# One store for the mLSTM state, and q evictions and output gates as woven tasks, in a one-core encoder step

## The chip, the cores and the metric

The kernel runs on one core of one Trainium2 chip. The metric is the device time of one execution in microseconds. The engines are named as in the profile: PE (TensorE, matmuls; PEld is its weight load), DVE (VectorE), ACT (ScalarE), POOL (GpSimd), and SP (SyncE), which here only issues DMAs. Each engine works off its own instructions in the order in which they stand in the program, and waits on semaphores for what they read.

## The reference: what is computed

One inference step of a two-layer encoder for a prompt of 1024 frames and a sample of 32 frames (1056 columns together), in float32, model width 1024. Layer 0 is an mLSTM (8 heads, key width 64, value width 128, chunks), layer 1 a sliding-window attention (16 query heads, 2 key/value heads). Both are followed by a SwiGLU feed-forward of width 2816. After each sub-layer comes x <- LayerNorm(alpha x + sublayer(x)).

The part that matters here is the mLSTM mixer:

```python
q, k, v, o, ig, fg = jnp.split(x @ w_in, A_SPLITS, axis=-1)
...
# per chunk, with the gates folded into d, w_inter, w_end, decay, m
qk = jnp.einsum('bhtd,bhsd->bhts', q, k) * d
num = w_inter[..., None] * jnp.einsum('bhtd,bhde->bhte', q, C0) + jnp.einsum('bhts,bhse->bhte', qk, v)
den = w_inter * jnp.einsum('bhtd,bhd->bht', q, n0) + jnp.sum(qk, -1)
h = num / jnp.maximum(jnp.abs(den), jnp.exp(-m))[..., None]
C_new = decay[..., None, None] * C0 + jnp.einsum('bhs,bhsd,bhse->bhde', w_end, k, v)
n_new = decay[..., None] * n0 + jnp.einsum('bhs,bhsd->bhd', w_end, k)
...
h = h * lax.rsqrt(jnp.mean(h * h, -1, keepdims=True) + HEAD_NORM_EPS)
h = h.reshape(B, T, H * M_DV) * g_norm * jax.nn.sigmoid(o)
return h @ w_out, C, n, m
```

The last C, n and m of the prompt and of the sample are outputs, beside the two y and some rows of K and V.

## The kernel before, in words

**Tiles.** The 1056 columns are cut into three groups of 384, 384 and 288 for the projections, and into nine chunks (eight of 128 columns for the prompt, one of 32 for the sample) for the mLSTM. The heads go in four pairs. Each float32 operand is split into a high and a low part, and each product is three matmuls (lines 582 to 584); these are called dense here. `d` is their PSUM tile, a ring of three banks in this stage. `wr` is a loaded weight of 512 KB, `wh` and `wl` its parts (lines 387 and 392; `oh` are further places for such parts), `sx` the parts of x.

**The mixer's stages.** For pair j the kernel projects q (three groups, each evicted to `qT` by ACT, line 894), k (evicted to `kT` by DVE, line 899) and v (nine chunks, evicted to `vt`). With v of pair 0 come the gates' raw values; `gate_task` turns them into rows of m and of weights (`scrm`, `scrw` in DRAM, lines 974 and 993), into columns, and last into the decays (PE line 1015). `mlstm` then runs one `item` per pair and chunk, 36 in all. An item loads `nm` and `wib` by broadcast DMAs from `scrm` and `scrw` (lines 1042 and 1046), copies q (POOL 1055, 1059), adds the mask to `nm` (POOL 1061), takes the exponential (ACT 1065), multiplies scores S = k q (PE 1075) by it into `p` (DVE 1080), forms H and the new state on PE (1098, 1100, 1102), updates C and n together as `Cn`, 128 x 129 (DVE 1122), normalises, and transposes the result (PE 1162) into `act`. Items 7 and 8 of a pair end the prompt's and the sample's state, and are stored with two DMAs each: C (128 rows of 128 elements, line 1130) and n (128 rows of one element, line 1131). After the four pairs `proj_o` projects the output gates o, takes the sigmoid by exponentials and logarithms, and multiplies it into `act`.

**What sets the order.** The program is straight-line code and the order on each engine is fixed when it is built. Some work is written as tasks (generators); `Weave` steps a task when a planner, `Clock`, thinks that its next instruction could start by the time PE gets there. `Clock` keeps a time for each engine and tile from fixed costs of each instruction. The stages around the tasks are plain code: `project` issues a group's dense matmuls and calls the tasks in between. `wv.until` and `wv.drain` step only tasks until a condition holds, so no dense matmul is placed meanwhile. Three such places bear on the change. Line 1192 holds q of pair j >= 2 until all nine items of pair j-2 are placed, because `qT` has two buffers. `begin` (line 1178) drains the gate task, opens a pool in the gates' room and starts `mlstm`; it is called after q and k of pair 1. And each `proj_o` pair waits for its items. SP issues all loads and stores in one queue, in the order in which they were placed.

Of the kernel before, what the change touches and what calls it, by code (L numbers as in the profile page):

```python
# [17 lines left out]
P = 128  # L18
# [6 lines left out]
HEADS = 8  # L25
# [39 lines left out]
class Clock:  # L65
# [70 lines left out]
    def see(self, i, *_):  # L136
# [13 lines left out]
        if op == "DMACopy":  # L150
# [291 lines left out]
def kernel(ctx: ExitStack, tc: tile.TileContext, A, O):  # L442
# [144 lines left out]
    def psbank():  # L587
        return new(psx[1][0], "d", [P, 512], F32, bufs=psx[1][1])

    def psdense(g):  # L590
        return psbank()[:, : GRP[g][1]]
# [13 lines left out]
    def project(u, g):  # L605

        ps = psdense(g)
        gemm(ps, wcols(u), xcols(g))
        return ps
# [419 lines left out]
    def mlstm():  # L1029
# [3 lines left out]
        def item(j, c):  # L1033
# [94 lines left out]
            else:  # L1128
                k = "p" if c == 7 else "s"
                nc.sync.dma_start(O[k + "_C"][2 * DK * j : 2 * DK * (j + 1), :], Cn[:, :DV])  # L1130
                nc.sync.dma_start(O[k + "_n"][2 * DK * j : 2 * DK * (j + 1), :], Cn[:, DV : DV + 1])
# [46 lines left out]
    def begin():  # L1178
        nonlocal pa2, task
        wv.drain(gtask)  # L1180
# [9 lines left out]
    for j in range(PAIRS):  # L1190
        if j > 1:
            wv.until(lambda: mst["done"] >= 9 * (j - 1))
        alloc_pair(j)
        if j:
            for g in range(3):
                proj_q(j, g)
            W.done(U_Q[j])
            for g in range(3):
                proj_k(j, g)
            W.done(U_K[j])  # L1200
        else:
            for g in range(3):
                proj_q(j, g)
                if g == 0:
                    W.split_to(U_V[0][0])
                if g == 2:
                    W.done(U_Q[j])
                    W.split_to(U_V[0][1])
                proj_k(j, g)
            W.done(U_K[j])  # L1210
# [7 lines left out]
    def proj_o(m, g, release):  # L1218
# [3 lines left out]
        if release:  # L1222
            W.done(U_O[m])
        t, r = scratch(m % 2, n)
# [26 lines left out]
    def scratch(i, n):  # L1251
        return [new(pa2, tag, [P, 384], bufs=2)[:, :n] for tag in ("sg", "sr")]
# [5 lines left out]
    wv.drain(task)  # L1258
    gn = base.tile([P, KT], F32, name="gn")
# [5 lines left out]
    def scratch(i, n):  # L1265
        return zz[:, 2 * i, :n], zz[:, 2 * i + 1, :n]

    for g in range(3):
        for m in range(6, 8):
            proj_o(m, g, False)  # L1270
# [713 lines left out]
def _arrays(i):  # L1984
# [49 lines left out]
    "p_C": (HEADS * DK, DV),  # L2034
    "p_n": (HEADS * DK, 1),
# [3 lines left out]
    "s_C": (HEADS * DK, DV),  # L2039
    "s_n": (HEADS * DK, 1),  # L2040
# [39 lines left out]
```

## Time and profile before

| | us |
|---|---|
| median of 3 runs | 2326.53 (2323.96 to 2331.42) |
| the profiled execution | 2327.41 |
| its span | 2325.6 |
| PE busy | 2239.0 (96%) |
| DVE busy | 1519.5 (65%) |
| ACT busy | 1030.2 (44%) |
| POOL busy | 793.7 (34%) |

Times in the profile are in us from the start of the span. A row of a timeline has the start, the duration, the engine and line, the operation with output and inputs, and in brackets how long the engine idled before it and what ended that. The stretch view gives each engine's busy time in a stretch, PE's granted clock (1.00 is full speed), the mean busy share of the 16 DMA engines, and what they moved. Roughly, the mixer's projections and mLSTM fill the first 400 us, layer 0's output projection and feed-forward the time to 1200, the attention 1250 to 1550, and layer 1's feed-forward the rest.

### The profile page before, as it was taken

The page shows a single profiled execution, that of the slowest core. Times are in us where ns is not written, and L with a number is a line of the kernel's source. Part 1 is how long each engine was busy: PE and PEld are TensorE (multiplying, and loading weights), DVE is VectorE, ACT ScalarE, POOL GpSimd, SP SyncE. Part 2 cuts the span into 40 slices and gives each one's busy share as a digit, 9 for nine tenths or more (in the row PEclk, how much of TensorE's full clock was granted, in tenths as well). Part 3 has the DMA queues.
Part 4 walks back from the last instruction along what each step waited for, and adds up shares of the span by engine and source line. Part 5 has one row for each costly group of instructions (what it writes and reads, how often), then busy time and mean ns, then how long its engine had stood idle before and what let it go on. Part 6 is the DMA issues. An engine that isn't in the chain of part 4 may idle for free.

```text
span 2325.6 us, 44258 instructions
## 1 busy us (share of the span) xinstructions
PE 2239.0 (96%) x17224; PEld 2182.8 (94%) x17224; DVE 1519.5 (65%) x3001; ACT 1030.2 (44%) x2300; POOL 793.7 (34%) x792
## 2 busy tenths in 40 slices
PE   8979999999999999999999899889999999999997
PEld 8868999999999999999998788889999999999997
DVE  4445456767766565666677767767766666566666
ACT  3334345555444444322257666656544444331233
POOL 1223210001545445444202545410244545444410
PEclk9979999999999999999999989989999999999999
DMA  4223221402434343698323100331244434389711
GB/s 144 67 49 53 64 29 55 139 19 73 167 121 167 139 158 121 236 328 264 118 82 110 48 31 21 105 115 37 74 167 158 149 126 161 103 287 329 246 57 66
DMA packets 165090, 289.71 MB, mean 125 GB/s; under 512 B 15824, under 2 KB 120840, under 8 KB 164880
## 3 DMA queue, kind: packets, MB, share of 16 engines
q1 hardware_dynamic: 160528, 282.56, 36.9%
q10 hardware_dynamic: 4352, 4.33, 0.5%
q8 instruction: 135, 2.21, 0.4%
q14 instruction: 75, 0.61, 0.1%
HBM read 203.89 MB, written 82.94 MB: 123 GB/s over the span
## 4 chain that ended last, share of the span: by engine, by line
PE 78%; DVE 8%; ACT 6%; DMA 4%; issue 3%; POOL 1%; SPq 0%; ACTq 0%; POOLq 0%; DVEq 0%
PE d L582 9%; PE d L583 9%; PE d L584 9%; PE A L582 8%; PE A L584 8%; PE A L583 8%; PE B L582 6%; PE B L583 6%; PE B L584 6%; PE ln L642 1%; PE T L1856 1%; PE H L1098 1%; ACT wh L387 1%; DMA hs_x<-z 1%; PE H L1100 1%
## 5 line engine op out<-in xcount | busy, mean ns | idle before, releaser
L392 POOL TENSOR_TENSOR wl<-wr,wh 128x512 fp32r<-128x512 f32 x406 | 574.2, 1430 | 915.7 <-ACT wh L387 831.9
L387 ACT CAST wh<-wr 128x512 fp32r<-128x512 f32 (+1 forms) x531 | 319.6, 617 | 477.0 <-DVE wr L361 264.7
L582 PE MATMUL A<-sx,wh 128*128 128x264 f32 x1280 | 364.5, 285 | 3.4 <-ACT z L1510 2.9
L583 PE MATMUL A<-sx,wh 128*128 128x264 f32 x1280 | 363.1, 284 | 0.0
L584 PE MATMUL A<-sx,wl 128*128 128x264 f32 x1280 | 363.1, 284 | 0.0
L582 PE MATMUL d<-sx,wh 128*128 128x264 f32 (+2 forms) x1092 | 345.9, 317 | 10.0 <-ACT sx L612 6.0
L583 PE MATMUL d<-sx,wh 128*128 128x264 f32 (+2 forms) x1092 | 337.4, 309 | 0.7 <-DVE sx L613 0.6
L584 PE MATMUL d<-sx,wl 128*128 128x264 f32 (+2 forms) x1092 | 336.5, 308 | 0.1
L582 PEld LDWEIGHTS A<-sx,wh 128*128 128x128 f32 x1280 | 240.6, 188 | 4.3 <-ACT z L1510 3.3
L584 PEld LDWEIGHTS A<-sx,wl 128*128 128x128 f32 x1280 | 241.2, 188 | 0.0
L583 PEld LDWEIGHTS A<-sx,wh 128*128 128x128 f32 x1280 | 240.7, 188 | 0.0
L582 PE MATMUL B<-ex,wh 128*128 128x264 f32 x832 | 236.5, 284 | 0.0
L583 PE MATMUL B<-ex,wh 128*128 128x264 f32 x832 | 236.0, 284 | 0.0
L584 PE MATMUL B<-ex,wl 128*128 128x264 f32 x832 | 235.8, 283 | 0.0
L582 PEld LDWEIGHTS d<-sx,wh 128*128 128x128 f32 x1092 | 210.4, 193 | 12.5 <-ACT sx L612 6.2
L583 PEld LDWEIGHTS d<-sx,wh 128*128 128x128 f32 x1092 | 210.4, 193 | 2.6 <-DVE sx L613 1.8
L584 PEld LDWEIGHTS d<-sx,wl 128*128 128x128 f32 x1092 | 209.8, 192 | 0.4 <-DVE wl L392 0.4
L582 PE MATMUL d<-sx,ex 128*128 128x264 f32 x612 | 177.3, 290 | 0.0
L584 PE MATMUL d<-sx,ex 128*128 128x264 f32 x612 | 173.7, 284 | 1.1 <-DVE ex L392 1.1
L1851 POOL TENSOR_SCALAR s<-s,st 128x256 f32<-128x256 f32 (+1 forms) x144 | 124.1, 876 | 146.1 <-DVE st L1848 126.6
L583 PE MATMUL d<-sx,ex 128*128 128x264 f32 x612 | 173.7, 284 | 0.0
L1376 DVE TENSOR_TENSOR z<-z 128x528 fp32r<-128x528 f32 x136 | 117.9, 880 | 69.8 <-ACT z L1374 69.4
(274 smaller groups left out, 5822.4 us busy)
## 6 DMA issues: line engine op xcount, KB each, us to landing
wr<-in_gu SPq DMA_DIRECT2D x96, 512.0 KB
hs_x<-z SPq DMA_DIRECT2D x72, 528.0 KB
hs_t<-z SPq DMA_DIRECT2D x64, 528.0 KB
sx<-hs_x SPq DMA_DIRECT2D x112, 264.0 KB
sx<-hs_t SPq DMA_DIRECT2D x64, 264.0 KB
ex<-hs_t SPq DMA_DIRECT2D x64, 264.0 KB
wr<-in_dn SPq DMA_DIRECT2D x32, 512.0 KB
ex<-hs_x SPq DMA_DIRECT2D x32, 264.0 KB
```

Source lines behind the costliest of these rows:

```text
L387: self.nc.scalar.copy(hi, r)
L392: eng.tensor_sub(lo, r, hi.bitcast(F32))
L582: nc.tensor.matmul(out, ah, bh, start=start and k == 0, stop=False, **kw)
L583: nc.tensor.matmul(out, ah, bl, start=False, stop=False, **kw)
L584: nc.tensor.matmul(out, al, bh, start=False, stop=stop and k == last, **kw)
L642: nc.tensor.matmul(t[:, :w], onesm[:], x[:, i, :], start=(i == 0), stop=(i == 1))
L1098: nc.tensor.matmul(ph[:L, h, :], p[:L, h, :L], vt[j][:L, c, h, :], start=True, stop=C is None)
L1100: nc.tensor.matmul(ph[:L, h, :], qw[:, h, :L], C[:], start=False, stop=True)
L1376: clk.sooner(2 * N4, hi).tensor_sub(lo.bitcast(F32R), buf(s), hi)
L1851: nc.gpsimd.tensor_scalar_mul(p[:R, h, lo:256], p[:R, h, lo:256], st[:R, 2, h : h + 1])
L1856: nc.tensor.transpose(pt[:nk, i, h, :R], p[:R, h, c : c + nk], ident[:R, :R])
```

## The change

It has four parts. The state matrix C and vector n, which lie together in `Cn`, leave in one store of 128 rows of 129 elements, and the host cuts them apart. The eviction of q is a task that waits for pair j-2 and holds its PSUM bank until it has run; the tiles of the pair are allocated in it. `begin` is a task that runs as soon as the gate task has ended. The output gates are a task for each group, which holds its PSUM bank until the first exponential, and holds its two scratch tiles to the end. Beside that three constants of the planner are other: a DMA whose rows are one element is costed at 8.5e-5 of the unit in which others have 0.1 to 0.39, an issue of a DMA takes 0.4 us of its engine in place of 0.06, and a result of 8 or 64 partitions no longer lets the next instruction of its engine overlap.

```diff
-            rate = 0.39 if row >= 2048 else 0.30 if row >= 1024 else 0.2 if row >= 512 else 0.1
+            rate = 0.39 if row >= 2048 else 0.30 if row >= 1024 else 0.2 if row >= 512 else 0.1 if row > 4 else 8.5e-5
             self.pipe = max(start + 1.3, self.pipe) + n / rate / 1e6
-            self.free[e] = start + 0.06
+            self.free[e] = start + 0.4
...
-            self.free[e] = end - self.LAP.get(e, 0.0)
+            part = outs and outs[0].ap[0][1] in (HEADS, 64)
+            self.free[e] = end + (0.014 if part else -self.LAP.get(e, 0.0))
...
-    def psbank():
-        return new(psx[1][0], "d", [P, 512], F32, bufs=psx[1][1])
...
+    def psbank(hold=False):
+        p, bufs = psx[1]
+        wv.until(ring(p, "d", bufs).open)
+        return new(p, "d", [P, 512], F32, bufs=bufs, hold=hold)
...
     def proj_q(j, g):
         t0, n = GRP[g]
-        ps = project(U_Q[j], g)
-        nc.scalar.copy(qT[j][:, t0 : t0 + n], ps)
+        t, ps = project(U_Q[j], g, True)
+
+        def out():
+            yield At("Activation", [ps], when=lambda: mst["done"] >= 9 * (j - 1))
+            if g == 0:
+                alloc_pair(j)
+            nc.scalar.copy(qT[j][:, t0 : t0 + n], ps)
+            release(psx[1][0], "d", t)
+
+        wv.launch(out())
 
     def proj_k(j, g):
         t0, n = GRP[g]
         ps = project(U_K[j], g)
+        if g == 0:
+            wv.until(lambda: j in qT)
...
-                nc.sync.dma_start(O[k + "_C"][2 * DK * j : 2 * DK * (j + 1), :], Cn[:, :DV])
-                nc.sync.dma_start(O[k + "_n"][2 * DK * j : 2 * DK * (j + 1), :], Cn[:, DV : DV + 1])
+                nc.sync.dma_start(O[k + "_Cn"][2 * DK * j : 2 * DK * (j + 1), :], Cn[:])
...
     def begin():
         nonlocal pa2, task
-        wv.drain(gtask)
+        yield At("SP", when=lambda: gtask not in wv.tasks)
...
     for j in range(PAIRS):
-        if j > 1:
-            wv.until(lambda: mst["done"] >= 9 * (j - 1))
-        alloc_pair(j)
...
             gtask = wv.launch(gate_task())
+            wv.launch(begin())
             W.ahead = True
         mst["ready"] = j + 1
+        proj_v(j)
         if j == 1:
-            begin()
-        proj_v(j)
+            wv.until(lambda: task)
...
+    def gate_out(m, g, bank, ps):
+        n = GRP[g][1]
+        rooms = [ring(pa2, tag, 2) for tag in ("sg", "sr")]
+        yield At("Activation", [ps], room=rooms)
+        both = [new(pa2, tag, [P, 384], bufs=2, hold=True) for tag in ("sg", "sr")]
+        t, r = (x[:, :n] for x in both)
+        nc.scalar.activation(t, ps, AF.Exp, scale=-1.0)
+        release(psx[1][0], "d", bank)
...
+        yield At("DVE", lambda: [t, h[:]], when=lambda: mst["done"] >= 9 * (m // 2 + 1))
+        nc.vector.scalar_tensor_tensor(h, h, gnorm[:, m : m + 1], t, op0=ALU.mult, op1=ALU.mult)
+        for tag, x in zip(("sg", "sr"), both):
+            release(pa2, tag, x)
...
     for m in range(6):
-        wv.until(lambda: mst["done"] >= 9 * (m // 2 + 1))
         for g in range(3):
-            proj_o(m, g, g == 2)
+            bank, ps = project(U_O[m], g, True)
+            gating.append(wv.launch(gate_out(m, g, bank, ps)))
+        W.done(U_O[m])
```

The order of instructions moves in three places of which the prediction speaks. The numbers in the rows are those of the tiles; the lines of the changed kernel are some 1 to 12 higher.

**The start of the mLSTM, on SP.** `Cs`, `nm` and `wib` are the first items' loads, `wr` a weight. Before:

```order
L993 DMA scrw_213<-wi_799 8x288
L995 DMA out_p_m<-m_798 8x1
L996 DMA out_s_m<-m_798 8x1
L343 DMA wr_912<-in_wqk 128x1024
L343 DMA wr_1004<-in_wv 128x1024
L343 DMA wr_1020<-in_wv 128x1024
L1039 DMA Cs_1046<-in_state_cn 128x129
L1042 DMA nm_1048<-scrm_208 128x2x128
L1042 DMA nm_1052<-scrm_208 128x2x128
L1046 DMA wib_1054<-scrw_211 64x128 x2
```

and now:

```order
L344 DMA wr_893<-in_wqk 128x1024
L1005 DMA scrw_213<-wi_816 8x288
L1007 DMA out_p_m<-m_815 8x1
L1008 DMA out_s_m<-m_815 8x1
L1051 DMA Cs_947<-in_state_cn 128x129
L1054 DMA nm_949<-scrm_208 128x2x128
L1054 DMA nm_953<-scrm_208 128x2x128
L1058 DMA wib_955<-scrw_211 64x128 x2
L1054 DMA nm_960<-scrm_208 128x2x128
L1058 DMA wib_962<-scrw_211 64x128 x2
L1054 DMA nm_1036<-scrm_209 128x2x128
L1058 DMA wib_1038<-scrw_212 64x128 x2
```

The two loads of wv stood ahead of the first item; they now follow the fourth. On PE the last gate matmul (line 1015) has 27 more dense matmuls ahead of it than before, and the first S stands 24 dense matmuls behind it, where 138 stood.

**The turn from pair 0 to pair 1, on SP.** Before:

```order
L1042 DMA nm_1598<-scrm_210 32x2x32
L1046 DMA wib_1600<-scrw_213 64x32 x2
L1130 DMA out_p_C<-Cn_1626 128x128
L1131 DMA out_p_n<-Cn_1626 128x1
L343 DMA wr_1650<-in_wqk 128x1024
L343 DMA wr_1664<-in_wqk 128x1024
L1130 DMA out_s_C<-Cn_1705 128x128
L1131 DMA out_s_n<-Cn_1705 128x1
L1039 DMA Cs_1714<-in_state_cn 128x129
L1042 DMA nm_1716<-scrm_208 128x2x128
```

and now:

```order
L1054 DMA nm_1476<-scrm_210 32x2x32
L1058 DMA wib_1478<-scrw_213 64x32 x2
L1051 DMA Cs_1538<-in_state_cn 128x129
L1054 DMA nm_1540<-scrm_208 128x2x128
L1142 DMA out_p_Cn<-Cn_1562 128x129
L1054 DMA nm_1609<-scrm_208 128x2x128
L1058 DMA wib_1611<-scrw_211 64x128 x2
L1142 DMA out_s_Cn<-Cn_1649 128x129
L1054 DMA nm_1679<-scrm_208 128x2x128
L1058 DMA wib_1681<-scrw_211 64x128 x2
```

The first broadcast of pair 1 stands ahead of the state's stores, and the two weight loads have gone from here; they follow the fourth item of pair 1.

**The end of pair 0, on PE.** `ht` is an item's result; its transposition is an item's last work on PE, and the 128x32 one is the last of the pair. Before:

```order
L1102 MATMUL T_1687<-vt_228,ks_1674 64x129 x2
L1162 MATMUL T_1702<-ident,ht_1697 128x128 x2
L1162 MATMUL T_1736<-ident,ht_1734 128x32 x2
L582 MATMUL d_1753<-sx,oh_102_996 128x384
L583 MATMUL d_1753<-sx,oh_102_996 128x384
L584 MATMUL d_1753<-sx,oh_103_997 128x384
```

and now:

```order
L583 MATMUL d_1729<-wh_765,sx 32x256
L584 MATMUL d_1729<-wl_766,sx 32x256
L585 MATMUL d_1729<-wh_765,sx 32x256
L1173 MATMUL T_1733<-ident,ht_1717 128x32 x2
L1087 MATMUL S_1742<-qz_215,kT_790 128x256
L1089 MATMUL T_1744<-ident,kT_790 128x128
```

Before, v of pair 1 (32x256 is its last chunk) was used up, and the last transpositions followed each other with q of pair 2 behind them. Now the pair ends inside v of pair 1, and items of pair 1 are already under way. The order also differs in the attention stage; in the feed-forward stages PE's order is as it was.

More of the change, by code (lines that the diff above doesn't have):

```diff
@@ L1190, with proj_o @@
     for j in range(PAIRS):
-        if j > 1:
-            wv.until(lambda: mst["done"] >= 9 * (j - 1))
-        alloc_pair(j)
+        for g in range(3):
+            proj_q(j, g)
+            if not j and g == 0:
+                W.split_to(U_V[0][0])
+            if g == 2:
+                W.done(U_Q[j])
+                if not j:
+                    W.split_to(U_V[0][1])
+            if not j:
+                proj_k(j, g)
         if j:
             for g in range(3):
-                proj_q(j, g)
-            W.done(U_Q[j])
-            for g in range(3):
                 proj_k(j, g)
[L1200 to L1210, printed above, removed]
+        W.done(U_K[j])
+        if not j:
             gtask = wv.launch(gate_task())
+            wv.launch(begin())
             W.ahead = True
         mst["ready"] = j + 1
+        proj_v(j)
         if j == 1:
-            begin()
-        proj_v(j)
-    def proj_o(m, g, release):
+            wv.until(lambda: task)
+    def proj_o(m, g):
         n = GRP[g][1]
         ps = project(U_O[m], g)
-        if release:
-            W.done(U_O[m])
-        t, r = scratch(m % 2, n)
+        t, r = (zz[:, 2 * (m % 2) + i, :n] for i in range(2))
         nc.scalar.activation(t, ps, AF.Exp, scale=-1.0)
@@ L2038 @@
     "p_v": (P, P),
-    "s_C": (HEADS * DK, DV),
-    "s_n": (HEADS * DK, 1),
+    "s_Cn": (HEADS * DK, DV + 1),
     "s_m": (HEADS, 1),
```

35 lines of the change are left out of this document (21 added, 14 removed).

## The prediction

> **What bounds the kernel now.** I read the page first, then busy time by stretch, then who waits in the worst stretch, then SP's queue in order of time.
>
> ```profile
> span 2325.6 us, 44258 instructions
> PE 2239.0 (96%) x17224; PEld 2182.8 (94%) x17224; DVE 1519.5 (65%) x3001; ACT 1030.2 (44%) x2300; POOL 793.7 (34%) x792
> ```
>
> TensorE (PE) is the bound: 2239.0 of 2325.6 us. The order of instructions has 16,577 rows for PE before and as many after, of the same shapes, so the change cannot make PE's work smaller. It can only take away PE's idle time (86.6 us) and the time in which PE runs at a lower granted clock. The next question is how much of either lies where the change acts. The columns below are the stretch, its length, busy time and count of PE, PEld, DVE, ACT and POOL, the granted clock, the DMA share and GB/s.
>
> ```profile
> 95.00:110.00 15.00, 11.76 (x81) 10.78 (x80) 3.93 (x17) 4.09 (x14) 6.60 (x14) 0.89 0.30 92
> 110.00:135.00 25.00, 24.89 (x203) 22.61 (x201) 16.22 (x73) 10.65 (x43) 10.61 (x27) 1.00 0.12 28
> 135.00:140.00 5.00, 3.48 (x30) 2.59 (x30) 2.73 (x15) 3.10 (x13) 0.00 (x0) 1.00 0.06 13
> 140.00:160.00 20.00, 9.12 (x33) 5.40 (x32) 6.90 (x27) 4.96 (x18) 2.98 (x8) 0.55 0.58 86
> 160.00:170.00 10.00, 9.81 (x47) 8.57 (x48) 3.77 (x19) 3.74 (x14) 4.96 (x11) 0.71 0.16 45
> 170.00:215.00 45.00, 45.00 (x328) 40.91 (x327) 24.70 (x108) 20.00 (x76) 13.37 (x33) 1.00 0.29 34
> 215.00:230.00 15.00, 12.48 (x98) 10.78 (x98) 7.91 (x38) 6.19 (x26) 9.09 (x22) 1.00 0.36 114
> 230.00:400.00 170.00, 170.00 (x1175) 161.39 (x1175) 96.58 (x315) 74.83 (x219) 24.94 (x60) 1.00 0.20 47
> ...
> 1250.00:1550.00 300.00, 263.89 (x1718) 243.60 (x1718) 211.44 (x734) 194.46 (x575) 132.86 (x169) 0.91 0.21 67
> 1460.00:1470.00 10.00, 6.14 (x29) 5.08 (x27) 8.18 (x29) 6.03 (x17) 5.40 (x6) 0.66 0.33 107
> ```
>
> The mLSTM stage runs from about 93 to 326 us. PE idles there at three places only: 95 to 110, 135 to 160, 215 to 230. These are the starts of pair 0, pair 1 and pair 2. From 230 to 400 us it has no idle time at all, so what the change does to the output gates has nothing to win there. The last two rows are the attention stage, which the new constants of the planner reorder; more of it below.
>
> Idle time in the mLSTM stage: 3.24 + 0.11 + 1.52 + 10.88 + 0.19 + 2.52 = 18.5 us. Clock: a PE busy for 9.12 us at 0.55 does what takes 9.12 x 0.55 at full clock, so it loses 9.12 x 0.45 = 4.1 us; likewise 11.76 x 0.11 = 1.3 and 9.81 x 0.29 = 2.8. Together 8.2 us. **The whole that can be won here is 26.7 us.**
>
> Who waits in the worst of it, 138 to 160 us (engine, line, what it waited for, total, times, longest):
>
> ```profile
> POOL nm L1061 <- DMA nm<-scrm: 11.3, 1, 11.3
> DVE p L1080 <- ACT nm L1065: 9.0, 1, 9.0
> ACT nm L1065 <- POOL nm L1061: 8.5, 1, 8.5
> ...
> PE T L1162 <- DVE ht L1156: 4.2, 2, 2.6
> ```
>
> PE waits for p, p for nm on ACT, that for nm on POOL, and POOL for a DMA: the broadcast of -m into nm. Ahead of that (140 to 150) PE only follows the last two items of pair 0 with no dense work between them, since line 1192 lets q of pair 2 begin when pair 0 is done. SP's queue in that stretch (start, duration of the issue):
>
> ```profile
> 138.81 0.43 SPq L1131 DMA_DIRECT2D out_p_n<-Cn  x1
> ...
> 140.99 1.96 SPq L343 DMA_DIRECT2D wr<-in_wqk  x2
> ...
> 147.41 0.42 SPq L1131 DMA_DIRECT2D out_s_n<-Cn  x1
> ...
> 148.41 1.06 SPq L1042 DMA_DIRECT2D nm<-scrm  x2
> ...
> 158.17 0.72 POOL L1061 TENSOR_TENSOR nm<-nm,cmask 128x256 f32<-128x256 f32 x1 [11.30 <-DMA nm<-scrm]
> ...
> 160.19 1.23 PE L1098 MATMUL H<-vt,p 128*128 128x129 f32 x4 [5.71 <-DVE p L1080]
> ```
>
> ```profile
> 142.00:143.00 1.00, 0.29 (x1) 0.00 (x1) 1.00 (x2) 0.54 (x2) 0.00 (x0) 0.50 2.85 82
> 143.00:149.00 6.00, 3.58 (x14) 1.30 (x14) 3.10 (x19) 1.54 (x7) 0.15 (x2) 0.50 0.29 35
> 149.00:153.00 4.00, 3.16 (x10) 2.94 (x11) 0.82 (x4) 0.19 (x1) 0.00 (x0) 0.50 1.22 295
> 153.00:158.00 5.00, 1.48 (x5) 0.87 (x3) 0.00 (x0) 0.00 (x0) 0.00 (x0) 0.50 0.37 37
> ```
>
> Two weight loads of 512 KB were issued at 141 to 143 us, yet the DMA engines move 35 GB/s until 149, and only then 295 GB/s. After that again 37 GB/s until nm lands at 158. Each of the slow stretches (6 and 5 us) stands right behind one of the two stores of n, 128 rows of 4 bytes each. I read them as about 5.5 us of queue time per store. A weight load alone does not explain 35 GB/s.
>
> **The change part by part.**
>
> *One store for C and n.* Eight issues of this row go; the eight C stores get one column more.
>
> ```profile
> L1131 SPq DMA_DIRECT2D out_p_n<-Cn x4: 424/432/881, 138.8 to 317.4; - x4
> ```
>
> That is 8 x 0.43 = 3.4 us of SP's issuing time, off the path by itself. What counts is the queue behind: 2 x 5.5 = 11 us at the turn to pair 1, in which nm, wib and the weights stand still. The trace has no store of 516-byte rows. Its bounds are the 0.34 us issue of a C store (nothing more behind it) and the 5.5 us of an n store; by form it is nearest to the C store, whose 512-byte rows it exceeds by one element, so I take nothing. The Trainium skill (DMA: Bandwidth & Descriptors, Specifications) says the same of the two sizes in its own terms: full rate from 512 B on, below that a read-modify-write; no run here shows yet whether 516 bytes keep to it.
>
> *begin() as a task, after the gates; q evicted by tasks.* Before, the mLSTM of pair 0 waits for all of q and k of pair 1:
>
> ```profile
> 77.07 1.06 PE L1015 MATMUL T<-dec,sel 8*128 8x9 f32 x8
> ...
> 91.10 1.81 SPq L343 DMA_DIRECT2D wr<-in_wv  x2
> ...
> 93.44 0.94 SPq L1042 DMA_DIRECT2D nm<-scrm  x2
> ...
> 97.68 0.59 PE L1075 MATMUL S<-qz,kT 128*128 128x256 f32 x2
> ...
> 98.11 0.27 PE L1077 MATMUL T<-ident,kT 128*128 128x128 f32 x1
> ...
> 100.67 0.72 POOL L1061 TENSOR_TENSOR nm<-nm,cmask 128x256 f32<-128x256 f32 x1 [6.58 <-issue]
> ...
> 102.69 0.71 PE L1098 MATMUL H<-vt,p 128*128 128x129 f32 x4 [3.24 <-DVE p L1080]
> ```
>
> In the new order the last gate matmul (L1015) comes 27 dense matmuls later and the first S 24 dense matmuls behind it. A dense matmul takes 0.16 us (row below), so the gates end at about 77.1 + 4.3 + 1.1 = 82.5 and S stands at 86.3 instead of 97.7. The broadcasts now leave before the two wv loads, not behind them. Here nm took 100.67 - 93.44 = 7.2 us with 1.05 MB ahead of it, which at 349 GB/s (row below) is 3.0 us; so 4.2 us without. From the gates' end: 0.8 us to the issue (an estimate: the copy of the decays, the hand-over to SP and the issue of Cs ahead), 4.2 to nm on POOL, then 2.0 (100.67 to 102.69) to H, 7.0 us. On PE between: (24 + 9) x 0.16 + 0.9 for S and T = 6.2 us. So I expect a wait of 0.8 us there, where there were 3.2.
>
> ```profile
> 350.00:400.00 50.00, 50.00 (x310) 50.00 (x310) 31.13 (x62) 23.90 (x49) 0.00 (x0) 1.00 0.16 51
> 215.00:218.00 3.00, 2.68 (x23) 2.25 (x22) 1.70 (x8) 0.24 (x2) 0.02 (x1) 1.00 1.01 349
> ```
>
> At the turn to pair 1 the chain of pair 0 ends inside v of pair 1, so dense work covers the 140 to 150 stretch. The new wait is in q's eviction: it holds a PSUM bank until pair j-2 is done, and behind it on ACT stand the weight splits. With three banks, PE can run q's 72 matmuls (11.5 us) past that wait before it stops; before, it could run none. Cost nothing; if the chain were later than that by x, PE would stop for x.
>
> The two wqk loads (pair 3's) move behind four items of pair 1. They are used some 70 us later.
>
> *Output gates in tasks.* Same instructions in number, on ACT and DVE, under a PE that is full from 230 to 400. Nothing; if the cover went, the 18 evictions would show, at 0.49 us each 8.9 us:
>
> ```profile
> L1225 ACT ACTIVATE sg<-d x18: 411/492/495, 325.0 to 390.8; 128x384 f32<-128x384 f32 x12, 128x288 f32<-128x288 f32 x6
> ```
>
> *The planner's constants* (0.4 us for a DMA issue, no overlap behind results of 8 or 64 partitions) reorder the attention stage too, where PE idles 36.1 us and runs at 0.91. A gap such as 1460 to 1470 costs 3.9 us idle and 6.14 x 0.34 = 2.1 us of clock, 6 us. The new order may make or mend such gaps; the bounds are two more and two fewer, 12 us either way. I take nothing, since both orders have much the same dense work between the steps. The feed-forward stages keep PE's order.
>
> **The sum.** 26.7 us can be won. I leave 0.8 at pair 0, and 2 us each at pairs 1 and 2 for the 1 MB of weights that still passes among the broadcasts (pair 2's idle 2.5 us is the row for that). 26.7 - 4.8 = 22. The profiled execution took 2327.4 us (span 2325.6 and 1.8 around it): 2305.4. The median of the runs is 0.9 lower, so **2305 us**.
>
> **Rivals.**
>
> *The weights, not the n stores, hold the broadcasts.* For it: 1 MB stood ahead of nm at all three places, and pair 0 lost 3.24 + 1.3 = 4.5 us with no n store about. Against it: 35 GB/s behind n stores. If each turn keeps 4.5 us, 13.5 of the 26.7 stay, and the time is 2327.4 - 13.2 - 0.9 = 2313. The Trainium skill (DMA: Bandwidth & Descriptors, Queues, rings and completion order) has each DMA engine take descriptors in ring order, which is this rival's mechanism: a load on SP's queue delays whatever SP issues after it. The trace agrees in so far as nm lands only after the loads issued ahead of it.
>
> *Attention comes out better by two gaps*: 2293.
>
> *Slower: attention loses more gaps than the mLSTM stage wins.* Place 1250 to 1550, price 6 us a gap; from the fourth gap on (24 against 22) the gain is gone, and from the fifth it is measurably slower. Six give 2305 + 36 = 2341, with DVE (211 of 300 us) and ACT (194) too loaded to catch up. Against it: the steps keep their number, and the constants added are nearer to the measured 0.43 us issue than those replaced.
>
> *It does not do what it says*: the bank held for q stops PE as long as line 1192 did, so 135 to 170 keeps its 1.5 + 10.9 + 4.1 + 2.8 = 19 us, and the time is 2322. The new order speaks against it: pair 0's last transposes stand before the end of v of pair 1.
>
> **How the numbers follow.** The forecast has 0.67 (own range 2297 to 2314), the weights 0.13, better attention 0.08, no effect 0.06, slower 0.06. A measurement of this kernel tells 0.3% (7 us) from no change: below 2319.5 is faster. Faster: nearly all of the first three, 0.84; the same: no effect and a little of the weights' case, 0.10; slower 0.06. For 8 in 10 the range takes in two better gaps at one end and the weights' case with one worse gap at the other: 2291 to 2320.
>
> **What would show it.** Right: no PE wait over 1.5 us at L1098 at the starts of pairs 1 and 2; clock 1.00 from 110 to 230; nm on POOL within 5 us of its issue; first S near 86 us; the mLSTM's last item about 22 us earlier; the attention's idle within 12 us of 36. Wrong: broadcasts that still take 8 to 10 us without the n stores; PE waiting for a bank (ACT qT) at q of pair 2; an attention with 50 us of idle.

## The result and the profile after

The changed kernel takes **2296.57 us** (median of 4 runs, 2296.23 to 2298.87), the kernel before 2326.60 beside it (2323.96 to 2331.42). The ratio is 0.9871, 95% interval 0.9853 to 0.9888: 30.0 us faster. The forecast was 2305, with a range of 2291 to 2320. So the sign and the range hold, and the gain is 8 us larger than the sum gave.

The page of the changed kernel:

```profile
span 2294.8 us, 44265 instructions
PE 2226.5 (97%) x17224; PEld 2175.6 (95%) x17224; DVE 1520.1 (66%) x3005; ACT 1029.1 (45%) x2300; POOL 787.3 (34%) x788
```

PE has the same 17,224 matmul records. Its busy time is 12.5 us shorter, because more of it runs at full clock, and its idle time fell from 86.6 to 68.3 us. The same stretches of the mixer as in the prediction, with the columns named there:

```profile
95.00:110.00 15.00, 15.00 (x124) 14.01 (x121) 11.23 (x47) 6.92 (x27) 6.48 (x15) 1.00 0.41 118
...
135.00:140.00 5.00, 5.00 (x41) 4.34 (x40) 3.54 (x15) 2.13 (x9) 4.34 (x12) 1.00 0.08 22
140.00:160.00 20.00, 20.00 (x136) 18.70 (x135) 11.47 (x46) 9.99 (x34) 8.22 (x20) 1.00 0.34 94
160.00:170.00 10.00, 10.00 (x70) 9.14 (x69) 5.56 (x28) 5.49 (x23) 1.77 (x8) 1.00 0.01 2
...
215.00:230.00 15.00, 15.00 (x106) 13.00 (x103) 9.62 (x41) 7.56 (x26) 0.92 (x5) 1.00 0.30 87
230.00:400.00 170.00, 169.80 (x1169) 163.92 (x1169) 101.76 (x281) 78.74 (x207) 20.17 (x45) 1.00 0.21 62
...
1220.80:1577.20 356.40, 318.37 (x2164) 298.61 (x2163) 257.82 (x817) 229.43 (x642) 133.27 (x169) 0.92 0.19 62
```

Where PE idled for 18.5 us and lost 8.2 us of clock, nothing is left: 0.2 us of idle time in 305 us, and a clock of 1.00 throughout. The last row is the attention, from the first score to the last item of its output projection; in it 38.0 us are idle. Before, that stretch read:

```profile
1248.90:1607.70 358.80, 322.29 (x2176) 300.95 (x2177) 256.79 (x814) 230.17 (x639) 135.52 (x171) 0.92 0.19 61
```

That is 36.5 us of idle time in 358.8. Where the 30.8 us between the two spans went, by the first or last start of a tile in each trace:

| place | before | after | gained up to here |
|---|---|---|---|
| last exponential of an output gate | 390.8 | 363.6 | 27.2 |
| first up-projection of layer 0's feed-forward | 563.0 | 534.2 | 28.8 |
| first score of the attention | 1248.9 | 1220.8 | 28.1 |
| last item of the attention's output projection | 1607.7 | 1577.2 | 30.5 |
| end of the span | 2325.6 | 2294.8 | 30.8 |

The starts of pair 0 and pair 1 in the changed kernel, from its timeline (SP's queue, POOL and PE):

```profile
81.32 0.94 SPq L1054 DMA_DIRECT2D nm<-scrm  x2
...
81.36 1.05 PE L1027 MATMUL T<-dec,sel 8*128 8x9 f32 x8
...
85.02 0.73 POOL L1073 TENSOR_TENSOR nm<-nm,cmask 128x256 f32<-128x256 f32 x1 [3.02 <-issue]
...
86.69 0.59 PE L1087 MATMUL S<-qz,kT 128*128 128x256 f32 x2
...
88.54 0.61 PE L1110 MATMUL H<-vt,p 128*128 128x129 f32 x4
...
124.79 0.34 SPq L1142 DMA_DIRECT2D out_p_Cn<-Cn  x1
125.24 0.38 SPq L1054 DMA_DIRECT2D nm<-scrm  x1
...
130.53 0.35 SPq L1142 DMA_DIRECT2D out_s_Cn<-Cn  x1
130.99 0.37 SPq L1054 DMA_DIRECT2D nm<-scrm  x1
...
131.90 0.61 PE L1110 MATMUL H<-vt,p 128*128 128x129 f32 x4
```

The first nm is on POOL 3.7 us after its issue (3.1 and 3.5 us for the first of pairs 1 and 2), and no H has a wait in brackets. All of PE's waits of any size from 60 to 440 us (engine, line, what it waited for, total, times, longest):

```profile
PE T L1173 <- DVE small L1158: 0.2, 1, 0.2
```

What remained open is which part brought how much, why the gain is larger than the sum, and what the attention's order has to do with it.

### The profile page after: what moved, and what is told of

It reads as the page before. It is cut to its first block, busy times and chain, and to the rows that moved or that the text cites. A ratio compares the mean times of both kernels' runs of the same rounds, so it can differ in the third digit from the quotient of the medians.

```text
span 2294.8 us, 44265 instructions
## 1 busy us (share of the span) xinstructions
PE 2226.5 (97%) x17224; PEld 2175.6 (95%) x17224; DVE 1520.1 (66%) x3005; ACT 1029.1 (45%) x2300; POOL 787.3 (34%) x788
## 4 chain that ended last, share of the span: by engine, by line
PE 86%; DVE 5%; DMA 3%; ACT 3%; issue 2%; POOL 1%; POOLq 0%; ACTq 0%; SPq 0%; DVEq 0%
PE d L583 11%; PE d L584 11%; PE d L585 11%; PE A L583 9%; PE A L584 9%; PE A L585 9%; PE B L583 7%; PE B L584 7%; PE B L585 6%; PE T L1882 1%; PE ln L644 1%; PE O L1899 1%; PE H L1110 1%; PE psS L1863 1%; PE S L1087 1%
## 5 line engine op out<-in xcount | busy, mean ns | idle before, releaser
L393 POOL TENSOR_TENSOR wl<-wr,wh 128x512 fp32r<-128x512 f32 (+1 forms) x401 | 566.3, 1428 | 826.8 <-ACT wh L388 740.9
L583 PE MATMUL d<-sx,ex 128*128 128x264 f32 x596 | 172.7, 290 | 0.0
L585 PE MATMUL d<-sx,ex 128*128 128x264 f32 x596 | 169.2, 284 | 0.0
L584 PE MATMUL d<-sx,ex 128*128 128x264 f32 x596 | 169.2, 284 | 0.0
L1402 DVE TENSOR_TENSOR z<-z 128x528 fp32r<-128x528 f32 x136 | 112.3, 837 | 74.3 <-ACT z L1400 73.5
```

Of the source, the lines that this page charges most:

```text
L393: eng.tensor_sub(lo, r, hi.bitcast(F32))
L583: nc.tensor.matmul(out, ah, bh, start=start and k == 0, stop=False, **kw)
L584: nc.tensor.matmul(out, ah, bl, start=False, stop=False, **kw)
L585: nc.tensor.matmul(out, al, bh, start=False, stop=stop and k == last, **kw)
L1402: clk.sooner(2 * N4, hi).tensor_sub(lo.bitcast(F32R), buf(s), hi)
```

## The experiments

"Before" in each group of runs was measured on the same chip: 2324.83 us for e1, e2, e5 and e7; 2324.58 for e3, e4, e6 and e8; 2326.10 for e9 to e12. Names: the *weave* is the new loop over the pairs with q's eviction and `begin` in tasks; the *constants* are the three of the planner.

### e1: the kernel before with one store

```diff
-                nc.sync.dma_start(O[k + "_C"][2 * DK * j : 2 * DK * (j + 1), :], Cn[:, :DV])
-                nc.sync.dma_start(O[k + "_n"][2 * DK * j : 2 * DK * (j + 1), :], Cn[:, DV : DV + 1])
+                nc.sync.dma_start(O[k + "_Cn"][2 * DK * j : 2 * DK * (j + 1), :], Cn[:])
```

> The kernel before with one edit: C and n leave in one store; the planner, the pairs' loop, begin and the gates are as before. Theory (the 4-byte rows of n hold SP's queue for about 5.5 us a store): nm of pair 1 lands within 5 us of its issue instead of 9.8, the wait of H at 160 us shrinks from 5.7 us to under 1, the turn to pair 2 loses its 2.5 us of idle, and the 140 to 150 stretch stays empty of dense work. Time about 2327 - 10 = 2316 us. Rival (the 1 MB of weights holds the broadcasts): nm still takes 8 us or more and the time is within 3 us of before.

2315.53 us (2314.93 to 2318.63), ratio 0.9965 (0.9951 to 0.9979): 9.3 us. PE's order of instructions is the same in all its rows as before, so this is the store alone. SP's queue, POOL and the stretches at the turn to pair 1:

```profile
144.79 0.90 SPq L1042 DMA_DIRECT2D nm<-scrm  x2
...
148.37 0.73 POOL L1061 TENSOR_TENSOR nm<-nm,cmask 128x256 f32<-128x256 f32 x1 [4.63 <-DMA nm<-scrm]
...
135.00:140.00 5.00, 1.26 (x7) 0.44 (x5) 4.34 (x14) 4.22 (x14) 1.16 (x2) 0.79 0.25 51
140.00:145.00 5.00, 3.58 (x14) 1.30 (x14) 2.32 (x14) 1.43 (x7) 0.15 (x2) 0.50 0.52 185
145.00:150.00 5.00, 3.29 (x11) 2.97 (x12) 1.47 (x8) 1.00 (x4) 1.56 (x3) 0.50 0.52 115
```

Two weight loads (137.86) still stand ahead of nm here, yet it takes 3.6 us in place of 9.8, and the queue moves 185 GB/s where it moved 35. The weights stand as far ahead of it as before (7 us). So it was the stores of n, not the weights, that held the broadcasts: the rival *weights hold the broadcasts* falls. The stretch with no dense work stays: 6.9 us idle between 135 and 150, at half clock.

### e2: the change with two stores

The e1 edit the other way round, in the changed kernel.

> The changed kernel with the two stores back (C and n apart), all else as changed, the planner knowing the price of one-element rows. Theory: the n stores again hold the queue for about 5.5 us each at the turns, but dense work now stands between, so PE loses 2 to 6 us: about 2300 us, with the broadcasts behind the n stores landing 5 us later than in the changed kernel. Rival (the weave alone made the gain): 2297 us, no difference.

2301.68 us (2301.09 to 2302.89), ratio 0.9905 (0.9889 to 0.9921): 5.1 us above the change, in the range expected. In its profile 3.6 of them have come by the first up-projection; PE's waits in the mixer sum up to 2.6 us, none over 1.2. The other 1.5 come in layer 0's feed-forward, and why is open. The broadcasts are not all late. At pair 1 the planner issues the next one only at 141.62, 9.8 us behind an n store. At pair 2 one goes out right behind such a store:

```profile
182.78 0.64 SPq L1143 DMA_DIRECT2D out_p_n<-Cn  x1
...
183.98 0.39 SPq L1054 DMA_DIRECT2D nm<-scrm  x1
...
194.58 0.73 POOL L1073 TENSOR_TENSOR nm<-nm,cmask 128x256 f32<-128x256 f32 x1 [21.36 <-DMA nm<-scrm]
```

It lands 10.4 us after its issue, and by way of POOL, ACT and DVE the next H waits 0.6 us for it; the longest landing of an nm that the change's trace records is 4.6 us. The trace also gives the two kinds of store their own price. Issues of the n and C stores in e2 with their durations in ns, and the time from issue to landing of the line (least, median, most):

```profile
L1143 SPq DMA_DIRECT2D out_p_n<-Cn x4: 423/424/637, 126.1 to 300.2; - x4
...
DMA to landing us min/median/max: 7.4/7.7/8.1
...
L1142 SPq DMA_DIRECT2D out_p_C<-Cn x4: 338/343/344, 125.7 to 299.8; - x4
...
DMA to landing us min/median/max: 1.5/1.5/5.0
```

and of the merged store in the changed kernel:

```profile
L1142 SPq DMA_DIRECT2D out_p_Cn<-Cn x4: 343/350/357, 124.8 to 296.3; - x4
...
DMA to landing us min/median/max: 1.8/1.9/3.5
```

Only three of the eight stores of each kind have their landing in the trace. By these, a store of 128 rows of 4 bytes takes 7.7 us to land, 6.2 more than 128 rows of 512 bytes; the 129th column in the same row costs about 0.4 us. The 5.0 us belong to a C store issued 5.4 us behind an n store. By the Trainium skill (DMA: Bandwidth & Descriptors, Specifications) rows under 512 bytes cost a read-modify-write and longer ones run at line rate; the three landing times fall on the two sides of that line as it says, but no run here shows the mechanism.

### e3: two stores, priced as before

As e2, and the planner prices one-element rows at 0.1 again.

```diff
-            rate = 0.39 if row >= 2048 else 0.30 if row >= 1024 else 0.2 if row >= 512 else 0.1 if row > 4 else 8.5e-5
+            rate = 0.39 if row >= 2048 else 0.30 if row >= 1024 else 0.2 if row >= 512 else 0.1
```

> The changed kernel with the two stores for each stream put back, and the planner pricing their 4-byte rows as before (0.1 of a byte per ns and engine instead of 8.5e-5). With the two stores alone the changed kernel took 2301.7 us, 5.1 more than the change, and its broadcasts of the next pair were then issued some 15 us after the n stores, out of their way. Theory: it was the planner's price that moved them away; without it the broadcasts are issued within 2 us of the n stores again, land 8 us or more after their issue, and PE waits at H (L1110) at the turns to pairs 1 and 2 for 3 us or more; the weave covers a part. So 2304 to 2308 us. Rival: the price moves nothing and the weave alone covers the wait: 2300 to 2303 us and waits at H under 2 us in sum.

2303.68 us (2303.67 to 2308.12), ratio 0.9921 (0.9906 to 0.9936), about 2 us above e2. From the timeline and the waits:

```profile
132.59 3.01 SPq L1054 DMA_DIRECT2D nm<-scrm  x1
...
179.57 3.08 SPq L1054 DMA_DIRECT2D nm<-scrm  x1
...
193.43 0.97 POOL L1071 TENSOR_TENSOR qwz<-qT,wib 64x128 f32<-64x128 f32 x2 [2.33 <-DMA wib<-scrw]
...
190.00:195.00 5.00, 2.63 (x19) 1.76 (x17) 0.00 (x0) 0.69 (x2) 2.46 (x6) 1.00 0.61 199
195.00:200.00 5.00, 4.01 (x23) 3.72 (x24) 1.83 (x11) 1.89 (x8) 2.87 (x8) 0.66 0.14 39
...
PE T L1089 <- DVE act L1179: 3.4, 1, 3.4
PE H L1110 <- DVE p L1092: 0.9, 1, 0.9
```

Both broadcasts are issued 0.5 us behind the issue of an n store, as the theory has it (at pair 2 e2 had one there too), and the issue itself stalls for 3 us. The trace records no landing for these two; POOL works on them 9.3 and 10.2 us after their issue. Two C stores issued 1.3 us behind an n store land after 8.6 and 8.9 us here, one with no n store near it after 2.1. PE's wait of 3.4 us stands at T, not at H, but a broadcast is behind it as well: T waits for a copy by DVE, that for one by ACT, which stands behind the exponential of nm; that waits for POOL, and POOL for wib. So the price is worth about 2 us when there are two stores; the expected 3 us came, but not at H. With one store nothing is left for it to price.

### e4: the change with plain output gates

```diff
+        wv.until(lambda: mst["done"] >= 9 * (m // 2 + 1))
         for g in range(3):
-            bank, ps = project(U_O[m], g, True)
-            gating.append(wv.launch(gate_out(m, g, bank, ps)))
-        W.done(U_O[m])
+            proj_o(m, g, plain, W.done if g == 2 else None)
```

> The changed kernel with the output gates of the first six units in plain code again (project, evict and gate in place, as before the change), all else as changed. Theory (the prediction's 'nothing'): in the stretch 230 to 400 us PE is full with or without the tasks, so the time stays within 3 us of the change: 2294 to 2300 us, and PE busy 49.8 or more in 250:300 and 300:350. Rival: the tasks carry the gain that the start of the mLSTM did not show, since the plain gates have to wait until the pair before them is done: 18 evictions of 0.49 us, 8.9 us, show on PE: 2304 to 2307 us, and the out-projection begins about 9 us later than in the changed kernel.

2299.81 us (2298.93 to 2304.49), ratio 0.9905 (0.9888 to 0.9922): 2 to 3 us above the change, within the theory's range. One wait comes back on PE between 230 and 430 us:

```profile
PE d L585 <- DVE ex L393: 1.1, 1, 1.1
```

The kernel before has the same one:

```profile
PE d L584 <- DVE ex L392: 1.1, 1, 1.1
```

So the gates' tasks are worth this 1.1 us, at the start of the output projection. The rest of the 2 to 3 us lies in the attention (357.5 us in place of 356.4), which has an order of its own in e4.

### e5: the change with the planner's old constants

```diff
-            rate = 0.39 if row >= 2048 else 0.30 if row >= 1024 else 0.2 if row >= 512 else 0.1 if row > 4 else 8.5e-5
+            rate = 0.39 if row >= 2048 else 0.30 if row >= 1024 else 0.2 if row >= 512 else 0.1
...
-            self.free[e] = start + 0.4
+            self.free[e] = start + 0.06
...
-            part = outs and outs[0].ap[0][1] in (HEADS, 64)
-            self.free[e] = end + (0.014 if part else -self.LAP.get(e, 0.0))
+            self.free[e] = end - self.LAP.get(e, 0.0)
```

> The changed kernel with the planner's three constants put back to those of before; store, pairs' loop, begin and gates as changed. Theory (the constants were not needed for the mLSTM stage, and move the attention by a few gaps of 6 us in either direction): PE idle between 80 and 300 us under 3 us, attention within 12 us of the changed kernel's, time 2290 to 2305 us. Rival (the constants made the mLSTM stage run without a wait): waits of 5 us or more come back at the starts of the pairs.

2292.26 us (2287.85 to 2294.32), ratio 0.9867 (0.9849 to 0.9885). From 100 to 300 us PE idles 0.4 us, so the rival falls. The change does not need the new constants; it is, if anything, faster without them. In the profiled run the mixer is 2.9 us slower (first up-projection at 537.1 in place of 534.2), and the attention takes 345.7 us in place of 356.4. That run is the fastest of the four, 2287.85 us, and the others took 2291.95 to 2294.32; how long their attention was is not recorded.

### e6: the kernel before with the new constants alone

The same three edits the other way round, in the kernel before.

> The kernel before with the planner's three constants of the change and nothing else (two stores, old order of the pairs, plain gates). Theory: the constants can only move broadcasts and stores out of each other's way; at the turn to pair 1 the order of the code still holds PE back, so the gain is at most what merging the stores alone gave (9.3 us): 2315 to 2325 us; the idle stretch 135 to 150 us stays. Rival: the constants carry the gain themselves, by the order in which the planner puts mLSTM and dense work: 2300 to 2310 us and no window under 4.5 us of busy PE between 130 and 160 us.

2309.98 us (2307.95 to 2312.12), ratio 0.9943 (0.9928 to 0.9958): 14.6 us. Neither theory holds. The gap that the order of the code makes is still there, as the first had it, so the second falls:

```profile
130.00:135.00 5.00, 1.86 (x15) 1.21 (x13) 3.29 (x13) 3.98 (x13) 0.00 (x0) 0.92 0.11 10
135.00:140.00 5.00, 3.73 (x17) 2.44 (x17) 3.54 (x15) 0.99 (x5) 0.00 (x0) 0.50 0.62 200
140.00:145.00 5.00, 4.08 (x18) 1.52 (x17) 2.21 (x13) 2.25 (x10) 0.15 (x2) 0.50 0.37 44
145.00:150.00 5.00, 3.11 (x12) 2.84 (x11) 1.47 (x8) 1.35 (x5) 1.44 (x4) 0.50 0.30 81
```

But the limit of 9.3 us that the first theory set was wrong as well. The first up-projection comes at 549.1 in place of 563.0, 13.9 us earlier, and the attention takes 352.9 us in place of 358.8. How the constants bring that is only partly seen. The start of pair 0 loses 0.8 us in place of 4.5, the turn to pair 1 13.4 in place of 19.5, and pair 2 nothing in place of 2.5. But at pairs 1 and 2 a broadcast still stands 1 us behind an n store on SP's queue (141.21 behind 140.22, 199.82 behind 198.83), so it is not that broadcasts were moved away from the stores.

### e7: the change with the old loop over the pairs

```diff
-        t, ps = project(U_Q[j], g, True)
...
-        wv.launch(out())
+        ps = project(U_Q[j], g)
+        nc.scalar.copy(qT[j][:, t0 : t0 + n], ps)
...
+        if j > 1:
+            wv.until(lambda: mst["done"] >= 9 * (j - 1))
+        alloc_pair(j)
...
-            wv.launch(begin())
...
+            begin()
+        proj_v(j)
```

> The changed kernel with the pairs' loop of before: q evicted in place, q of pair j held until pair j-2 is done, begin after k of pair 1. One store, gate tasks and planner as changed. Theory: the stretch without dense work at the end of pair 0 comes back (about 6 us idle and 3 us of clock) and the start of pair 0 waits for its broadcasts behind the wv loads (about 3 us): 2296.6 + 10 = 2307 us. Rival (only the store mattered): within 3 us of the changed kernel.

2312.31 us (2311.71 to 2313.62), ratio 0.9951 (0.9935 to 0.9967): 15.7 us above the change, where some 10 were expected. The gap is back:

```profile
130.00:135.00 5.00, 2.02 (x16) 1.33 (x15) 3.33 (x13) 3.63 (x13) 0.61 (x2) 1.00 0.00 0
135.00:140.00 5.00, 3.33 (x15) 2.56 (x16) 3.62 (x16) 1.00 (x4) 0.00 (x0) 0.66 0.68 210
140.00:145.00 5.00, 4.07 (x18) 1.36 (x17) 2.41 (x14) 2.26 (x11) 0.52 (x1) 0.50 0.51 92
145.00:150.00 5.00, 4.60 (x16) 2.97 (x16) 2.13 (x10) 2.11 (x8) 3.25 (x8) 0.50 0.40 92
150.00:155.00 5.00, 3.92 (x18) 2.90 (x17) 3.17 (x15) 2.19 (x9) 4.22 (x12) 0.50 0.14 41
```

7.1 us idle, and 15.9 us of busy time at 0.5 to 0.66 of the clock, which loses 0.34 x 3.33 + 0.5 x 12.6 = 7.4. Together 14.5, nearly all of the 15.7. The wait of about 3 us that was expected at the start of pair 0 is 1.5, at full clock. Since the n stores are gone in this kernel, this is what the weave itself removes.

### e8, e12: old constants from the end of the mixer on

The constants of the change up to the last output gate, those of before from there to the end. Both runs are the same kernel.

```diff
+    OLD = False
...
-            rate = 0.39 if row >= 2048 else 0.30 if row >= 1024 else 0.2 if row >= 512 else 0.1 if row > 4 else 8.5e-5
+            rate = 0.39 if row >= 2048 else 0.30 if row >= 1024 else 0.2 if row >= 512 else 0.1 if row > 4 or self.OLD else 8.5e-5
...
-            self.free[e] = start + 0.4
+            self.free[e] = start + (0.06 if self.OLD else 0.4)
...
-            self.free[e] = end + (0.014 if part else -self.LAP.get(e, 0.0))
+            self.free[e] = end + (0.014 if part and not self.OLD else -self.LAP.get(e, 0.0))
...
+    clk.OLD = True
     gn = base.tile([P, KT], F32, name="gn")
```

> The changed kernel with the planner's new constants up to the last output gate of the mixer, and the constants of before from there to the end. With the old constants throughout, the attention (first score to last out-projection of its mixer) took 345.7 us instead of 356.4, and the mixer 2.9 us more. Theory A: each stage's time goes by the constants in force in that stage: mixer as in the changed kernel (first up-projection of the feed-forward at 534 us), attention 346 us, 2284 to 2288 us, better than both. Theory B: the attention's order hangs on the whole state that the planner arrives with, and the constants have no sign: an attention anywhere from 346 to 360 us, so 2285 to 2300 us; a value over 352 us speaks for B.

> The changed kernel with the constants of before from the end of the mixer on, a second time, to be compared with the change on the same chip: if its 8 us are its own, 2286 to 2291 us and intervals that do not touch; if not, both within 3 us of one another.

> The changed kernel itself, beside the next one on the same chip: 2294 to 2299 us.

e8: 2288.39 us (2286.07 to 2289.39), ratio 0.9849 (0.9834 to 0.9864), with the first up-projection at 535.3 and an attention of 346.4: what theory A forecast, and theory B allows it. e12: 2286.51 us (2284.67 to 2289.54), ratio 0.9827 (0.9807 to 0.9847), beside the change itself (e11) at 2297.54 (2296.53 to 2298.31) on the same chip: 11 us less, and the ranges do not touch. **This version beats both kernels.** (Lines of e12 are 3 higher than those of the change.) The attention of e12, from the first score to the last item of its output projection, and two of PE's waits in it:

```profile
1221.30:1569.10 347.80, 315.70 (x2176) 297.20 (x2177) 255.00 (x815) 228.43 (x639) 133.26 (x170) 0.93 0.19 63
...
PE O L1901 <- ACT hi L1891: 8.8, 8, 3.7
...
PE T L1885 <- POOL s L1880: 2.5, 7, 0.6
```

and of e11, the change:

```profile
1219.90:1576.70 356.80, 318.54 (x2164) 298.77 (x2163) 257.95 (x816) 229.40 (x642) 133.32 (x169) 0.92 0.19 62
...
PE T L1882 <- POOL s L1877: 9.9, 17, 2.0
PE O L1898 <- ACT hi L1888: 7.9, 6, 2.6
```

The 9.0 us between them are 6.2 of idle time (38.3 and 32.1) and 2.8 of busy time. The wait of the transpositions for the scaled scores of POOL differs most: 9.9 us in 17 waits against 2.5 in 7.

### e9, e10: which constants the attention goes by

e9 is e8 the other way round (old constants in the mixer, new ones after it). e10 is e8 with only the last of the three put back after the mixer.

> The counterpart: the planner's old constants up to the last output gate of the mixer, the new ones from there to the end. Theory A (each stage goes by the constants in force in it): mixer as with the old constants throughout (first up-projection of the feed-forward at 537 us), attention as in the changed kernel (356 us): 2296 to 2301 us. Theory B (the attention's order hangs on the state with which the planner arrives): the attention lies anywhere from 346 to 360 us; under 352 us speaks for B.

> The changed kernel with only one of the three constants put back from the end of the mixer on: an engine counts as free before the end of an instruction on 8, 32 or 64 partitions again (the change put 0.014 us behind the end). The price of 4-byte rows and of SP's issue stay as changed. With all three put back there the kernel took 2288.4 us and the attention 346.4 us. Theory A1: in the attention it is this constant that decides, since its instructions on 64 partitions stand on ACT and DVE throughout: 2286 to 2291 us, attention 344 to 349 us. Rival: it is the issue price of SP (0.06 or 0.4 us), and this one does nothing: 2294 to 2299 us, attention 353 to 359 us.

e9: 2297.10 us (2294.03 to 2297.91), ratio 0.9869 (0.9850 to 0.9888). The time lies in theory A's range and the mixer ends at 537.7 as A has it, but the attention takes 352.7: neither 356 nor under 352, so it does not decide. e10: 2291.80 us (2290.41 to 2292.82), ratio 0.9847 (0.9825 to 0.9868), attention 351.0, between the bounds of both theories.

What decides more is the whole set. The attention's length in the profiled runs, with runs that have word for word the same order on PE from there to the end put together:

| order of the attention on PE | constants there | attention, us |
|---|---|---|
| before, e1 | old | 358.8, 359.9 |
| change, e11, e2, e3, e7 | new | 356.4, 356.8, 356.5, 355.9, 355.6 |
| e4 | new | 357.5 |
| e6 | new | 352.9 |
| e9 | new | 352.7 |
| e10 | one old, two new | 351.0 |
| e8, e12 | old | 346.4, 347.8 |
| e5 | old | 345.7 |

In these executions the same order gives the same length within 1.4 us, and eight orders spread over 14 us. (e5 is one execution, and its fastest.) Old constants stand at both ends of the table and new ones at four places in between. So the length goes with the order, and the order hangs on the state with which the planner arrives as well as on its constants: e6, e9, e4 and the change share the constants there and have four orders. For the changed code the old constants gave the two best orders; two are too few to make that a rule. What in the planner's state turns one order into another stays open.

## Why the prediction was right, and where its sum was off

**The place and the size of what can be won: right.** The sum found 26.7 us in the mixer, at three places, by idle time and clock. 27.2 us came out of the mixer up to the last output gate, and the stretches read 15.00 of 15.00, 20.00 of 20.00 and so on at a clock of 1.00. The match is in part luck, though. Of the 26.7, 4.5 us lay at the start of pair 0, and e1, e6 and e7, which start that pair with the same DMAs ahead of it, lose only 1.1, 0.8 and 1.5 us there. So 3 us or more of the 26.7 were not set by the order that the change mends; whether other executions of the kernel before lose them is not recorded.

**"5.5 us of queue time per store": right.** The landing time of 7.7 us against 1.5 is 6.2 us per store, and e1 gained 9.3 us where 2 x 5.5 = 11 were counted. That e1 gained it as the sum put it is only partly so. In its profile the mixer up to the last output gate is 14.5 us shorter, and 3.5 of these are lost again behind it. The turn to pair 1 gave 8.2 us: 12.6 us of idle and 6.9 of clock became 6.9 and 4.4 (135 to 170 us, with 0.7 of e1's clock loss from 150 to 155, where it reads 0.85). Pair 2 gave its 2.5 us of idle time. Another 3.4 us came at pair 0, where no n store is near. There nm took 5.1 us from issue to POOL in place of 7.2 with the same DMAs ahead of it. The old profile shows an issue of wib that stalled for 4.03 us at that place; why is open.

**The start of pair 0: right to 0.4 us.** The gates ended on PE at 81.36 + 1.05 = 82.4 (82.5 forecast), the first S came at 86.7 (86.3), and nm was on POOL 3.7 us after its issue (4.2). The wait of 0.8 us at H did not come, since nm is issued 1.1 us before the gates' end, not 0.8 after it: the broadcast does not need the decays.

**The q eviction that holds a bank: right.** No wait of PE for ACT's qT shows up, and e7 puts the weave at 15.7 us.

**The residual of 4.8 us: the step that failed.** "I leave 0.8 at pair 0, and 2 us each at pairs 1 and 2" measured 0 at all three. The 2 us were taken from pair 2's idle 2.5 us, as the price of the weights. But e1, with the weights where they were, has no PE wait at pair 2 at all, so the weights alone do not cost that. Neither does an n store ahead of the broadcast: e6 has one there, and PE is busy for all 30 us from 200 to 230. What made the 2.5 us in the old profile stays open. The row was read as the price of one cause while another stood ahead of it in the same queue.

**Output gates "nothing": off by 1.1 us**, the one wait at the output projection that e4 brings back. It stood just behind 400 us, outside the stretch that the prediction read.

**The attention "nothing, 12 us either way": right as a bound, and 2.4 us better.** The runs spread over 14 us, as wide as two or three gaps, and e5 lies 13.1 us below the kernel before, outside the 12. That the order of the change came out so near to the old one is luck: the term was the largest unknown of the case, and the reading "both orders have much the same dense work between the steps" did not see that an order 9 to 11 us better lies as near as three constants. The idle time stayed within 12 us of 36, at 38.0.

The difference of 8.8 us between the forecast gain and that of the spans is then 5.2 in the mixer (4.8 of residual and 0.4 not traced), 1.6 up to the feed-forward (1.1 of it the gates' wait), -0.7 in layer 0's feed-forward, 2.4 in the attention and 0.3 behind it.

**One mark was badly chosen.** "The mLSTM's last item about 22 us earlier": its last transposition moved from 337.1 to 302.8, 34 us. In e4, with plain gates, it stands at 314.7, and the last output gate at the same 363.6: so 12 us of the shift come with the gates' tasks and move nothing behind them. The last output gate, 27.2 us earlier, was the right place to look.

Of the rivals, *weights* fell with e1. *Does not do what it says* fell with e7: where the loop is the old one, the gap at 130 to 155 us is there, and in the change it is not. *Slower by the attention* and *better by two gaps* did not occur in the change; e5, e8 and e12 came near the second, with attentions 9 to 11 us shorter.

The parts do not add: the store alone 9.3, the constants alone 14.6, and taken out of the change the weave 15.7, the store 5.1, the gates some 3, while without the constants it is 4 us faster. The store and the constants cover in part the same gaps as the weave (the starts of the pairs), so that each of them is worth more alone than as the last one added.

## What to carry to other kernels

Where a load on a queue is late, look at what was issued just ahead of it on the same queue, and ask for each transfer by itself how long it takes to land: here a store of 512 bytes in all took longer to land than a load of 512 KB (7.7 us against 5.1 in the page's list of DMA issues), and merging it into its neighbour's rows cost about 0.4 us. A price for what is left over should not be taken from a row at which two causes stand in one queue. Where a planner sets the order, one build is one draw: with the same work the attention lay anywhere in 14 us, so a change to the planner's constants should be tried stage by stage, and each stage's order kept where it is best.

## What the runs showed of the hardware

- 128 rows of 4 bytes from the chip's working memory to DRAM land 7.4 to 8.1 us after issue (8.3 to 9.2 in e3), 128 rows of 512 bytes in 1.5 (median), and 128 rows of 516 bytes in 1.9; each figure rests on three landings in a trace. While the 4-byte store is under way, what is issued behind it on the same queue hardly moves (35 and 37 GB/s in the kernel before; in e3 C stores behind one land after 8.6 and 8.9 us in place of 2.1), and the next issue itself can stall for 3 us (e3).
- The granted clock fell behind long waits: e3's wait of 3.4 us is followed by a stretch at 0.66, while e2's two waits at H, of at most 1.2 us, leave every 5 us from 100 to 200 at 1.00. One long wait is not needed: in e1 from 135 to 150 no wait is over 2.6 us, but PE is busy for only 8.1 of 15 us, and the clock falls to 0.50. The Trainium skill (TensorE: Matmul & The Clock Gate, Part 1: The HAM clock gate) has half the clock after an idle window of about 3.4 us. The 3.4 us of e3 agree; the kernel before also lost clock after a wait of 3.24 us (0.89 over 95 to 110), a little under that window.
- With the same DMAs ahead of it in the same order, the first broadcast took 4.7, 5.1, 5.5 and 7.2 us from its issue to POOL (e6, e1, e7 and the kernel before). A single profile can be off by that much at one place.
